# Decay factors loaded as rows, three small loads moved, and the last squares taken in place, in a hybrid gMLP and state-space decoder kernel

## The chip, the cores and the metric

The kernel runs on one core of a Trainium2 chip. The metric is the device time of one execution in microseconds; of the kernel before, three runs took 1399.7 to 1400.92 us, with a median of 1400.12 us. A separate execution with the hardware profiler gives the profile.

## The reference, cut to what matters

One layer works on x of 1024 tokens by 1024 features, all in float32. A conditioning vector c gives a shift, a scale and a gate. The normalized and modulated input h is multiplied by `w_in` (1024 x 11296), and its columns feed two branches: a gMLP branch (y_a) and a Mamba-2 state-space branch (y_b). The branches are projected, gated, added and projected once more.

```python
adt = dt * a                                   # per token and head, 32 heads
a_cs = jnp.cumsum(adt, axis=-1)                # within chunks of 128 tokens
decay = segsum_exp(adt)                        # exp(a_cs[i] - a_cs[j]) for i >= j, else 0
cb = jnp.einsum('bclgn,bcsgn->bcgls', cc, bc)
y_diag = jnp.einsum('bcgls,bcgrls,bcsgrp->bclgrp', cb, decay, xd)
...
y_off = jnp.einsum('bclgn,bcgrpn,bcgrl->bclgrp', cc, prev_states, jnp.exp(a_cs))
return (y_diag + y_off).reshape(b, s, h, p).astype(x.dtype)
...
y_b = y_b + xh * d_skip[:, None]
yz = (y_b.reshape(b, s, SSM_D_INNER) * jax.nn.silu(ssm_z)).reshape(b, s, SSM_GROUPS, ...)
y_b = rms_norm(yz, ssm_norm_w.reshape(SSM_GROUPS, -1)).reshape(b, s, SSM_D_INNER)
merged = jax.nn.sigmoid(g_a) * (y_a @ w_proj_a) + jax.nn.sigmoid(g_b) * (y_b @ w_proj_b)
return x + gate[:, None, :] * (merged @ w_out)   # then a last rms_norm
```

The `jnp.exp(a_cs)` in `y_off` is what the change is about: one number per token and head, by which the part of y that comes from the state is multiplied.

## The kernel before, in words

The kernel is written as a sequence of stages in which TensorE is to be fed without a break. Large products are cut into quadrants (seven products in place of eight), and each float32 operand is split into a high part (a cast) and a low part (a subtraction), so that each product is made three times. A framework places the instructions of the engines: what is wrapped in `pin` (`tc.keep_in_program_order`) keeps its order on its engine; everything else is put by the framework's own schedule where it expects the operands to be ready, be it much earlier than the place in the code. Each engine then works strictly in its order. Loads go out from SyncE (`load`, L89, in program order), stores from ScalarE's queue (`store`, L92). A tile that takes the place of an older one (same tag) waits until all readers of the older one are through.

The stages, with their times in the profile:

1. **First products (0 to 73 us).** For n = 0 to 7 the kernel makes a column block of the modulation (`matvec`, L254, from the weights `aw`), transposes x, and makes the rows of h: `modulation` (L271 to 278) adds on VectorE, `rows_of_h` (L287) on ScalarE, and `first_products` (L322) multiplies them on TensorE. At n = 1, `dtb`, `abc` and `dsk` are loaded (L457 to 460): 32 numbers each, broadcast to 128 partitions. `dsk` is first needed in `small_parameters2` (L495), which copies it into `dskt` (L503); `dtb` and `abc` in the dt part, near 690 us. Which task runs when is written as slots: `later(25, small_parameters)` (L1268) means 25 products on.
2. **The projections (73 to 918 us).** `v_block` and then pairs of column blocks of `w_in`. Beside them, in small tasks, the softplus of dt and the sums are made (`dt_part1` to `dt_part3`, L641 to 717). `dt_part3` puts the running sums a_cs, heads on partitions, into `act` (32 x 1024) and stores them in DRAM as `acs_d`.
3. **The state-space stage (918 to 1146 us).** There are 32 steps: 8 groups of 4 heads by 4 pieces of 256 tokens, in the order of L1241. For a step, `fetch` (L1080) loads `dcy`, the sums of the 4 heads broadcast to all partitions, and `sl` (B, C, x and z of the piece), into one of 5 sets of buffers. `decay` (L1096) first makes `ea` = exp of the sums on ScalarE (L1101, two instructions of 64 partitions, heads of even and of odd number), then masks `dcy` in place on GpSimd (L1104), then takes 8 exponentials (L1109). `prep` makes transposes and the products with the decay (L1129), `front` multiplies (`yi`, `sp`) and carries the state `st` on (L1157 on GpSimd, L1159 on VectorE), and `back` multiplies the state (`yn`) and lets `evacuate` (L1176) put y together: `ym` = `yn` x `ea` (L1189), then on GpSimd the sum (L1190) and the product with z (`yz`, L1191). Between these, TensorE is filled with pieces of y_a times `w_proj_a` (`proj_a`, L1397): a generator, of which `draw(n)` takes n pieces of two matmuls, 192 in all, 24 for a block of rows. Its weights are cast (`wah`, L1316) and subtracted (`wal`, L1317) beside it. A step's order is front, draws, back, prep of two steps on, fetch of six on, decay of four on (L1461 to 1471).
4. **The norm of y_b.** `post` (L1193) stores `yz` in DRAM and, for most groups, squares it five slots later (`squares`, in place) and sums over channels with the matmuls `pq` in `post2` (L1213). For the second half of the last two groups it squares at once into new tiles `sq` (L1203), whose tags are those of `ea` (`ea_r`) and of `ym` or `y1`. Their `post2` stands behind `draw(left[0] - 5)` (L1477 to 1479), when 5 pieces of `proj_a` are left.
5. **Projection of y_b (from 1160 us).** Units (`p1`, k) and so on, L1532. A unit has `loads` (a norm row `rb`, `yn` = y_b from DRAM, weights `p1r`), `operands` (norm, cast, subtraction on VectorE and ScalarE) and `multiply` (L1585): 12 matmuls into 4 PSUM banks x0 to x3 or y0 to y3. `loads` of six units and `operands` of four run ahead (L1681). The first `rb` tile takes the first tag of `ea_r` (L1480, L1515 to 1517), the first `yn` tiles take tags of the state and of `proj_a`'s operands. The banks take the places of those of the stage before, in the order of L1709.
6. **The last product with `w_out`, the residual and the final norm (to 1403 us).**

## Time and profile before

| | |
|---|---|
| median of 3 runs | 1400.12 us |
| the profiled execution | 1404.41 us, of which its span is 1402.7 us |
| mean granted TensorE clock | 0.993 |
| TensorE, VectorE, ScalarE, GpSimd busy | 98%, 74%, 57%, 13% of the span |
| moved by DMA | 288.60 MB, 206 GB/s over the span |

In the rows, PE is TensorE (PEld its weight loads), DVE VectorE, ACT ScalarE, POOL GpSimd, SP SyncE; ACTq and SPq are the queues from which an engine issues DMAs. "L1104" is a line of the kernel. A row of the timeline has a start and a length in us, the engine, the line, output and inputs by name, shapes, and in brackets how long the engine stood idle before and what ended that. A row of the waits has the engine, its instruction, the instruction or DMA it waited for, and then the sum in us, the number of times and the longest. A row of the windows view has the stretch, its length, and for PE, PEld, DVE, ACT and POOL the busy time with the number of instructions, then the granted clock, the DMA engines' share and GB/s. A row of groups or of a tile has durations in ns. A busy TensorE is not one at its peak: at a granted clock of 0.5 it is as busy and half as fast.

### The profile page before, as it was taken

Reading aid. Unit: us, or ns where it says so; the run is one execution under the profiler, and the core shown is the slowest. Engines: PE = TensorE matmul, PEld = TensorE weight load, DVE = VectorE, ACT = ScalarE, POOL = GpSimd, SP = SyncE. Lnnn points to the kernel's source line nnn. Section 1 sums busy time; section 2 is a strip of 40 time slices with the busy share of each in tenths; the row PEclk is TensorE's granted clock in tenths of the full one; section 3 lists DMA queues with packets and bytes.
Section 4 is the critical chain, followed back from the end, with each engine's and each line's share of the span. In section 5 each row is a group of like instructions: output and inputs, shape, how many; then the busy total and the mean of one; then the engine's idle time right before and its main releaser. Section 6 shows DMA issues by size and latency. Waiting matters only on the chain.

```text
span 1402.7 us, 20203 instructions
## 1 busy us (share of the span) xinstructions
PE 1370.8 (98%) x6951; PEld 1133.6 (81%) x6951; DVE 1041.7 (74%) x1724; ACT 800.0 (57%) x1447; POOL 189.1 (13%) x191
## 2 busy tenths in 40 slices
PE   8999999999999999999999999999999999999997
PEld 6588888888888888888888888888888877788786
DVE  4685876777778789788888885398777736859976
ACT  4664666667556566465576555677666714233443
POOL 1000000000000000000000000038868760000002
PEclk9999999999999999999999999999999999999999
DMA  8674534343435667787675764698787719978913
GB/s 265 176 234 137 151 120 121 100 126 118 130 99 148 195 196 246 229 260 210 196 218 177 234 205 139 212 362 305 270 272 266 266 65 323 346 250 298 381 63 120
DMA packets 247228, 288.60 MB, mean 206 GB/s; under 512 B 14509, under 2 KB 194133, under 8 KB 247125
## 3 DMA queue, kind: packets, MB, share of 16 engines
q1 hardware_dynamic: 173716, 203.76, 45.5%
q10 hardware_dynamic: 73408, 83.54, 17.5%
q8 instruction: 55, 0.90, 0.3%
q14 instruction: 49, 0.39, 0.1%
HBM read 199.79 MB, written 87.46 MB: 205 GB/s over the span
## 4 chain that ended last, share of the span: by engine, by line
PE 69%; DMA 11%; DVE 8%; ACT 4%; issue 3%; SPq 2%; POOL 2%; ACTq 0%; DVEq 0%; POOLq 0%
PE xz L565 6%; PE xx L565 6%; PE xg L565 5%; PE xcb L565 5%; PE xuz L565 5%; PE pma L81 3%; PE vx L954 3%; PE yx L565 3%; PE yz L565 3%; PE ycb L565 3%; PE yg L565 3%; PE ox L1775 2%; PE yuz L565 2%; SPq L90 2%; DMA yn<-yb_d 2%
## 5 line engine op out<-in xcount | busy, mean ns | idle before, releaser
L1104 POOL TENSOR_SCALAR_AFFINE_SELECT dcy<-dcy 128x1024 f32<-128x1024 f32 x32 | 35.0, 1092 | 794.6 <-DMA yl<-ya_d 748.6
L1109 ACT ACTIVATE dcy<-dcy,nacs 128x128 f32<-128x128 f32 x256 | 78.5, 388 | 14.1 <-POOL dcy L1104 13.7
L1101 ACT ACTIVATE ea<-dcy 64x512 f32<-64x512 f32 x64 | 40.1, 626 | 13.0 <-DMA dcy<-acs_d 12.5
L1189 DVE TENSOR_TENSOR ym<-yn,ea 128x512 f32<-128x512 f32 (+1 forms) x32 | 19.9, 622 | 32.8 <-PE yn L81 32.8
L81 PE MATMUL pma<-yh,wah 128*128 128x512 f32 x128 | 43.9, 424 | 0.0
L1129 DVE TENSOR_TENSOR dcy<-dcy,pc 128x1024 f32<-128x1024 f32 x32 | 38.9, 1217 | 5.0 <-PE pc L84 4.0
L81 PE MATMUL pma<-yh,wal 128*128 128x512 f32 x128 | 42.6, 414 | 0.0
L1024 ACT ACTIVATE ac<-ac 128x1024 f32<-128x1024 f32 x32 | 34.0, 1061 | 13.5 <-DVE ac L1022 13.2
L1191 POOL TENSOR_TENSOR yz<-y,sl 128x512 f32<-128x512 f32 x32 | 41.4, 1293 | 0.9
L81 PE MATMUL pma<-yl,wah 128*128 128x512 f32 x128 | 40.3, 396 | 0.0
L1530 DVE SCALAR_TENSOR_TENSOR yn<-yn,par,rb 128x512 f32<-128x512 f32 x32 | 23.8, 747 | 21.7 <-DMA yn<-yb_d 21.7
L1190 POOL TENSOR_TENSOR y<-y,ym 128x512 f32<-128x512 f32 (+1 forms) x32 | 36.5, 1142 | 14.6 <-DVE ym L1189 14.6
L81 PEld LDWEIGHTS yn<-sl,st 128*128 128x128 f32 x224 | 30.2, 191 | 8.4 <-POOL yz L1211 2.5
L81 PE MATMUL sp<-xe,bn 128*128 128x256 f32 x112 | 33.7, 418 | 3.1 <-DVE ssq L1221 1.6
L81 PE MATMUL yi<-dcy,xd 128*64 128x128 f32 x512 | 35.9, 284 | 0.7 <-DVE st L1159 0.7
L81 PE MATMUL yn<-sl,st 128*128 128x128 f32 x224 | 31.1, 276 | 5.2 <-DVE st L1159 5.2
L1790 POOL TENSOR_TENSOR r<-r,fnw 128x512 f32<-128x512 f32 x4 | 5.3, 1334 | 228.6 <-ACT junk L1788 228.6
L1022 DVE SCALAR_TENSOR_TENSOR ac<-c2x,cwt,ac 128x1023 f32<-128x1023 f32 (+2 forms) x24 | 30.7, 1280 | 6.2 <-ACT ac L1020 6.1
L1022 DVE SCALAR_TENSOR_TENSOR ac<-c2cb,cwt,ac 128x1023 f32<-128x1023 f32 (+2 forms) x24 | 30.6, 1275 | 5.6 <-ACT ac L1020 5.5
L824 ACT CAST wbb<-wbr 128x512 fp32r<-128x512 f32 x32 | 19.8, 619 | 26.1 <-DMA wb_d<-wbb 20.5
L986 ACT ACTIVATE vm<-vm,vr 128x128 f32<-128x128 f32 x64 | 25.8, 484 | 14.9 <-DMA vm<-v_d 10.3
L1157 POOL TENSOR_TENSOR st<-st,cd 128x256 f32<-128x256 f32 x48 | 32.9, 685 | 9.7 <-PE yn L81 6.3
(2974 smaller groups left out, 4385.3 us busy)
## 6 DMA issues: line engine op xcount, KB each, us to landing
sl<-s_d SPq DMA_DIRECT2D x32, 768.0 KB
s_d<-ac ACTq DMA_DIRECT2D x32, 512.0 KB
wb_d<-wbb ACTq DMA_DIRECT2D x32, 512.0 KB
dcy<-acs_d SPq DMA_DIRECT2D x32, 512.0 KB
av<-in_w_in_dram SPq DMA_DIRECT2D x36, 256.0 KB
aw<-in_ada_w_dram SPq DMA_DIRECT2D x16, 512.0 KB
wbr<-in_w_proj_b_dram SPq DMA_DIRECT2D x32, 256.0 KB
yb_d<-yz ACTq DMA_DIRECT2D x32, 256.0 KB
```

The source lines that it names most:

```text
L81: pin(PE.matmul(acc, l, r, start=first, stop=last))
L565: pin(PE.matmul(ps, lw[:, k * P : (k + 1) * P], r[k], start=first and n + k == 0, stop=n == 2 and k == 3, skip_group_check=not first))
L954: pin(PE.matmul(ps[pn][j], l[:, j * P : (j + 1) * P], r, start=nm in ("p1", "p5", "p2") and n + units[i][1] == 0, stop=n == 2 and k == 3, ...
L1022: V.scalar_tensor_tensor(ac[:, s:], cc[:, : S - s], conv_wt[:, 3 - s, i : i + 1], ac[:, s:], op0=ALU.mult, op1=ALU.add)
L1024: A.activation(ac, ac, AF.Silu)
L1101: A.activation(ea[hh * HD : (hh + 1) * HD], dcy.rearrange("p (j e) i l -> p e j (i l)", e=2)[hh * HD : (hh + 1) * HD, hh], AF.Exp)
L1104: G.affine_select(out=d8, in_=d8, compare_op=ALU.is_ge, fill=-1e30, base=0, pattern=[[0, 2 * HPG], [1, P]], channel_multiplier=-1)
L1109: A.activation(dcy[:, h, i, :], dcy[:, h, i, :], AF.Exp, bias=sub[:, i, h : h + 1])
L1129: V.tensor_tensor(d3, d3, pc[:, 0:256].unsqueeze(1).to_broadcast([P, HPG, 256]), op=ALU.mult)
L1157: G.tensor_mul(v3(s2), v3(self.st), fac(cd, g, s)[:, i].unsqueeze(2).to_broadcast([P, HPG, HD]))
L1190: G.tensor_add(y1[:, :, t0:], y1[:, :, t0:], m[:, :, t0:])
L1191: G.tensor_mul(yz, y1, sl[:, 4:6])
```

## The change

It has four parts.

- The exponentials of the sums are made once: two tasks follow `dt_part3`. `dt_part4` takes the exponential of `act` in place (32 x 1024, one instruction), and `dt_part5` stores it in DRAM as `eas_d`, in 16 stores, sorted by even and odd heads. `fetch` loads each step's `ea` as two broadcast loads of 64 partitions x 512, behind `sl`; the two exponentials at the head of `decay` are gone.
- The loads of `dtb`, `abc` and `dsk` move from n = 1 of the first products to the head of `small_parameters`.
- The late squares are made in place in `yz`, five slots after `post`, and not in new tiles. `post2` of group 6 stands where 8 pieces of `proj_a` are left, ahead of the first loads of `p1`; that of group 7 stands where 3 are left, after the loads of the fourth unit and the operands of the second.
- The eight first PSUM banks of stage 5 are named in another order.

```diff
     acs_d = dt_([NG, 4, HPG, 256], "acs_d")
+    eas_d = dt_([NG, 4, 2, HPG // 2, 256], "eas_d")
...
-                if at == 1 and n == 1:
-                    load(dtb, dt_bias.to_broadcast([P, NH]))
-                    load(abc, a_log.to_broadcast([P, NH]))
-                    load(dsk, d_skip.to_broadcast([P, NH]))
...
     def small_parameters():

+        load(dtb, dt_bias.to_broadcast([P, NH]))
+        load(abc, a_log.to_broadcast([P, NH]))
+        load(dsk, d_skip.to_broadcast([P, NH]))
         pkb = wide("pkb").rearrange("p (i q) -> p i q", q=P)
...
+        later(2, dt_part4, act)
+
+    def dt_part4(act):
+        A.activation(act, act, AF.Exp)
+        later(2, dt_part5, act)
+
+    def dt_part5(act):
+        for g in range(NG):
+            for e in range(2):
+                store(eas_d[g, :, e].rearrange("s j t -> j s t"),
+                      act[HPG * g + e : HPG * (g + 1) : 2, :].rearrange("h (s t) -> h s t", s=4))
...
                 ea = turn(ea_r, f"ea{nm}", F32).rearrange("p (j t) -> p j t", j=2)
+            for hh in range(2):
+                load(ea[hh * HD : (hh + 1) * HD],
+                     eas_d[g, s, hh].rearrange("j t -> (j t)").unsqueeze(0).to_broadcast([HD, 512]))
             self.pre[s] = (sl, dcy, ea)
...
             sl, dcy, ea = self.pre[s]
-            for hh in range(2):
-                A.activation(ea[hh * HD : (hh + 1) * HD],
-                             dcy.rearrange("p (j e) i l -> p e j (i l)", e=2)[hh * HD : (hh + 1) * HD, hh], AF.Exp)
...
-                self.late = sq = [turn(r, f"sq{g}", F32) for r in (ea_r, (ym_r, y1_r)[g % 2])]
-                for j in range(2):
-                    pin(A.activation(sq[j], yz[:, j], AF.Square))
-                G.tensor_add(sq[0], sq[0], sq[1])
+                self.late = [yz[:, j] for j in range(2)]
+                later(5, self.late_squares)
+
+        def late_squares(self):
+            sq = self.late
+            for j in range(2):
+                pin(A.activation(sq[j], sq[j], AF.Square))
+            G.tensor_add(sq[0], sq[0], sq[1])
...
-    draw(left[0] - 5)
-    for late in groups[NG - 2 :]:
-        late.post2(1, late.late[:1])
     room.extend(ea_r[0] + [st_r[0][1]])
...
+    draw(left[0] - 8)
+    groups[6].post2(1, groups[6].late[:1])
     for u in range(LOAD):
         loads(u)
         if u > 1:
             operands(u - 2)
+        if u == 3:
+            draw(left[0] - 3)
+            groups[7].post2(1, groups[7].late[:1])
...
-                first = {t: psb.tile([P, 512], F32, name=f"{t}p", tag=f"b{t}") for t in ('y0', 'y2', 'x0', 'x1', 'y1', 'x2', 'y3', 'x3')}
+                first = {t: psb.tile([P, 512], F32, name=f"{t}p", tag=f"b{t}") for t in ('y2', 'y1', 'x0', 'x1', 'x2', 'x3', 'y0', 'y3')}
```

## The prediction

> **What bounds the kernel now.** I read the page first, then busy time by stage (one call of the windows view), the waits, and the timeline around each place where TensorE stands still.
>
> ```profile
> span 1402.7 us, 20203 instructions
> ...
> PE 1370.8 (98%) x6951; PEld 1133.6 (81%) x6951; DVE 1041.7 (74%) x1724; ACT 800.0 (57%) x1447; POOL 189.1 (13%) x191
> ```
>
> TensorE is busy for 98% of the span: 1402.7 - 1370.8 leaves 31.9 us of idle. The change takes no product away, so a gain can come only from those 31.9 us and from stretches in which matmuls run at a lower granted clock. So the question is which pauses the edits reach. By stage (length, busy us of PE, PEld, DVE, ACT, POOL, then granted clock, DMA share, GB/s):
>
> ```profile
> 36.00:72.00 36.00, 33.87 (x232) 21.59 (x233) 25.43 (x54) 26.07 (x47) 0.00 (x0) 0.95 0.60 178
> ...
> 120.00:882.00 762.00, 761.37 (x3423) 629.83 (x3422) 591.50 (x923) 460.42 (x712) 1.30 (x2) 1.00 0.57 173
> ...
> 918.00:960.00 42.00, 41.95 (x292) 35.07 (x291) 35.92 (x61) 31.29 (x80) 23.20 (x25) 1.00 0.94 327
> 960.00:1000.00 40.00, 39.37 (x299) 34.36 (x298) 31.20 (x56) 32.46 (x86) 32.78 (x32) 1.00 0.82 289
> 1000.00:1040.00 40.00, 36.52 (x277) 32.25 (x276) 28.55 (x55) 25.63 (x65) 29.86 (x29) 0.96 0.75 253
> 1040.00:1080.00 40.00, 37.53 (x286) 32.50 (x286) 28.62 (x53) 26.92 (x72) 34.29 (x35) 1.00 0.81 282
> 1080.00:1120.00 40.00, 38.71 (x304) 34.06 (x303) 29.14 (x56) 28.05 (x73) 30.67 (x30) 1.00 0.83 286
> 1120.00:1140.00 20.00, 18.35 (x132) 15.53 (x130) 11.28 (x22) 2.51 (x5) 14.05 (x13) 0.91 0.07 26
> ...
> 1152.00:1162.00 10.00, 5.44 (x27) 3.98 (x27) 3.36 (x7) 2.27 (x4) 3.25 (x2) 0.81 0.74 253
> ...
> 1172.00:1182.00 10.00, 10.00 (x45) 8.24 (x45) 5.25 (x10) 2.36 (x5) 0.00 (x0) 1.00 0.81 258
> ```
>
> The projections (120 to 882) lose 0.6 us in 762: nothing is to be won there, and there is little to be seen if ACT gets more to do. Three places lose time: the first products (36 to 72: 2.1 us idle and a clock of 0.95), the state-space stage (918 to 1140: 0.05 + 0.63 + 3.48 + 2.47 + 1.29 + 1.65 = 9.6 us idle, and clocks of 0.96 and 0.91 in two windows), and the passage from `proj_a` to `p1` (1152 to 1162: 4.6 us idle, clock 0.81). The edits touch all three, so I price them one by one.
>
> **Edit A: the three small loads leave the first stage.** Start, length, engine, instruction, and what ended the idle time before it:
>
> ```profile
> 32.14 0.50 PE L81 MATMUL pm<-ones,row 128*128 128x1 f32 x4
> ...
> 36.28 0.35 DVE L503 COPY dskt<-dsk 64x16 f32<-64x16 f32 x2 [4.35 <-DMA dsk<-in_d_skip_dram]
> ...
> 37.86 0.73 PE L81 MATMUL acc<-b11h,w0h 128*128 128x512 f32 x2 [2.60 <-ACT b11h L300]
> ...
> 38.52 1.90 PE L81 MATMUL pm<-aw,scz 128*32 128x256 f32 x16
> ```
>
> ```profile
> 38.00:40.00 2.00, 2.00 (x18) 0.76 (x18) 1.45 (x3) 1.81 (x3) 0.00 (x0) 0.65 0.24 75
> 40.00:42.00 2.00, 2.00 (x10) 1.55 (x7) 1.81 (x4) 1.20 (x3) 0.00 (x0) 0.50 0.12 28
> ```
>
> VectorE's queue holds the copies `dskt<-dsk` (L503). The code asks for them far later, but they aren't kept in program order and stand here, in front of the modulation add (L275) of step n = 2. That add's input was there at 32.14 + 0.50 = 32.64. VectorE instead sat 4.35 us for the landing of `dsk`; behind it waited L275, ACT's `b11h`, and TensorE, which stood for 2.60 us. The next windows show a granted clock of 0.65 and 0.50: 2.0 x 0.35 + 2.0 x 0.50 = 1.7 us lost. With the loads gone, L275 can go at about 32.7, which is 4 us sooner, and `b11h` is ready by about 33.8, before TensorE is through with the products it has (35.26 = 37.86 - 2.60). So A is worth 2.60 + 1.7 = **4.3 us**. Bounds: 0, if another operand is late at the same place, and 4.3. I take the upper end, because ACT and VectorE move forward by the same 4 us and `w0` and `aw` for this step were already in use or landed. At their new place (ahead of `pkb`) the loads have no buffer to wait for, and the copies meet the projection stage, whose 0.6 us idle in 762 shows the cover; without it the price would be the 4.35 us again.
>
> By the Trainium skill, page "TensorE: Matmul & The Clock Gate", section "What's actually happening", the clock falls after an idle window of about 3.4 us; by that rule a 2.60 us pause costs nothing more, A would be 2.6 and the whole 1387. The trace disagrees (0.50 granted right behind a pause of 2.60), and I go by the trace.
>
> **Edit B: the squares of the last groups and the order around `p1`.**
>
> ```profile
> SPq L90 <- PE pq L81: 38.0, 1, 38.0
> ```
>
> ```profile
> 1152.67 0.32 SPq L90 DMA_DIRECT2D rb<-rs_d  x1
> ...
> 1155.30 0.63 PE L81 MATMUL pma<-yh,wal 128*128 128x512 f32 x2
> ...
> 1160.49 0.80 PE L1592 MATMUL x0p<-p1bh,p1a 128*128 128x512 f32 x1 [4.56 <-ACT p1a L1572]
> ...
> 1164.88 0.46 PE L1592 MATMUL x3p<-p1bh,p1a 128*128 128x512 f32 x1
> ```
>
> SyncE issues `rb<-rs_d`, the first load of `p1`, at 1152.67, after 38.0 us of waiting on the matmuls `pq`. The reason is a buffer: the first `rb` tile takes the first tag of `ea_r`, and the old code put the late squares `sq` there, which are read by `pq` at the very end. All of `p1`'s loads stand in line behind it. So TensorE ends `proj_a` at 1155.30 + 0.63 = 1155.93 and waits 4.56 us for `p1`'s first operands. Then the clock is down: each j of a unit has three products (L1590 to 1593), so the first `x3p` is the tenth, and nine took 1164.88 - 1160.49 = 4.39 us; at the rate of 1172 to 1182 (45 in 10 us, 0.222 each) they need 2.0. B costs 4.56 + 2.4 = **6.9 us** now.
>
> After the change the squares overwrite `yz`, the `ea_r` tags are free with the last `ym`, and the first loads hang on tags that `proj_a` gives back: `yh` of k = 0 in its last row block is read in the first 3 of 24 draws, so 21 draws of two products (21 x 2 x 0.222 = 9.3 us) before the end at least. From the first issue to `x0p` it takes 1160.49 - 1152.67 = 7.8 us now, so 9.3 do. What can be late next:
>
> ```profile
> L1205 ACT ACTIVATE sq<-yz x4: 615/623/631, 1140.1 to 1146.8; 128x512 f32<-128x512 f32 x4
> L1206 POOL TENSOR_TENSOR sq<-sq,sq x2: 1279/1283/1287, 1142.9 to 1147.5; 128x512 f32<-128x512 f32 x2
> ```
>
> The squares must now wait for the store of `yz` (behind them on ACT stand `p1`'s casts), then come 2 x 0.623 on ACT and 1.283 on POOL. They begin at 1140.1 and 1146.8 now, 15.8 and 9.1 us before 1155.93, and `pq` is asked for at 8 and 3 draws (3.6 and 1.3 us) before the end instead of 5: about 5 us are left for the later store. The subtractions of unit 0 on VectorE stand behind the first `pq`'s scaling (both kept in order); two of 0.69 (as that of L1317 below) fit in 3.6 us. The PSUM banks are renamed so that no `x` bank is one which `proj_a` still fills. I see nothing left to wait for and take 6.9; the bounds are 0 (another wait of the same length) and 6.9. The later units run at full rate already (10.00 busy of 10.00).
>
> **Edit C: `ea` comes by DMA.**
>
> ```profile
> L1101 ACT ACTIVATE ea<-dcy 64x512 f32<-64x512 f32 x64 | 40.1, 626 | 13.0 <-DMA dcy<-acs_d 12.5
> ```
>
> ```profile
> POOL dcy L1104 <- ACT ea L1101: 46.0, 20, 16.6
> ...
> ACT ea L1101 <- DMA dcy<-acs_d: 12.5, 9, 2.5
> ...
> PE yn L81 <- DVE st L1159: 5.2, 3, 2.4
> ```
>
> Removed: 64 exponentials of 626 ns, 40.1 us of ACT, 1.25 us per step of 32. POOL's mask (L1104) stands behind both, since it overwrites what they read: it waited 46.0 us for them in 20 cases (16.6 of that in one). Now it waits only for the load of `dcy`, for which ACT waited 12.5 us in 9 cases. None of that is on TensorE's path by itself. What reaches TensorE is the order within ACT, and two of its pauses (of the three behind `st`, 5.2 us together) show it:
>
> ```profile
> 996.81 0.69 DVE L1317 TENSOR_TENSOR wal<-wa,wah 128x512 fp32r<-128x512 f32 x1 [1.65 <-ACT wah L1316]
> ...
> 1002.02 0.68 PE L81 MATMUL yn<-sl,st 128*128 128x128 f32 x4 [1.13 <-DVE st L1159]
> ```
>
> ```profile
> 1072.47 1.26 ACT L1101 ACTIVATE ea<-dcy 64x512 f32<-64x512 f32 x2
> ...
> 1074.93 0.76 DVE L1317 TENSOR_TENSOR wal<-wa,wah 128x512 fp32r<-128x512 f32 x1 [2.14 <-ACT wah L1316]
> ...
> 1079.61 0.57 PE L81 MATMUL yn<-sl,st 128*128 128x128 f32 x3 [1.69 <-DVE st L1159]
> ```
>
> At 1074.93 VectorE waits 2.14 us for the cast `wah`, which stood on ACT behind the two `ea` of 1072.47 (1.26 us); the update `st`, queued behind it on VectorE, then lets TensorE wait 1.69 us. At 996.81 it is the same with 1.65 and 1.13 us. With ACT 1.26 us earlier both nearly vanish: 1.13 + 1.26 = 2.4 us at least. The rest of the 9.6 us are pauses of 0.6 to 2.4 us in which ACT has a part, or none; I count a quarter of it (7.2 x 0.25 = 1.8) and none of the clock loss (40 x 0.04 + 20 x 0.09 = 3.4). C gains about **4 us**. Bounds: everything, 9.6 + 3.4 = 13.0, and below nothing, since transfers are added.
>
> Added: two loads of 128 KB a step, a kind that before doesn't have, 8.4 MB in all. Their price is bounded by nothing (hidden) and by what rival 5 asks; the nearest rows give the middle. At 286 GB/s with DMA busy for 0.83 of the time, a full queue moves 345 GB/s, so a step's two loads cost 0.76 us of DMA in a step of about 6.9 us, and the share goes from about 0.8 to 0.91. For issues, and for the single steps near 750:
>
> ```profile
> L93 ACTq DMA_DIRECT2D acs_d<-act x8: 253/366/748, 745.1 to 748.7; - x8
> ```
>
> ```profile
> 748.59 1.28 ACT L1024 ACT_TABLE_LOAD   x1 [0.52 <-DMA acs_d<-act]
> ...
> 749.88 1.06 ACT L1024 ACTIVATE ac<-ac 128x1024 f32<-128x1024 f32 x1
> ```
>
> SyncE issues 64 more, at ACT's 0.366 each 23 us, on a queue that mostly waits for buffers here. `ym` on VectorE now needs that load and no longer ACT; behind it would wait `st` and the next `dcy` product. A new `ea` waits for the `ym` of five steps before; the `sl` load just ahead of it waits for POOL's `yz` of that step, which follows `ym`, so no wait is added, but the next `dcy` load is behind two more issues and 0.76 us of transfer. It has cover: the mask leads its products by 20 us and more (rows in rival 5).
>
> Once: an exponential of 32 x 1024 on ACT (1.06 us for the same length), up to two table loads of 1.28, and 16 stores at 0.366, 5.9 us. The 8 stores of `acs_d` (745.1 to 748.7) left no mark on TensorE in that stage. I take 0; without the cover it is 5.9 + 1.06 + 2.56 = 9.5.
>
> **Sum.** 4.3 + 6.9 + 4 = 15.2 us. The profiled execution took 1404.41 us (span 1402.7, 1.7 around it), so it would take 1389.2. The median of the runs shown, 1400.12, lies 4.3 us lower; I take the sum from it: **1385 us**. About 0.2% (2.8 us) is what a measurement of this kernel can tell from no change.
>
> **Rivals.**
> (1) C gives nothing or a little less than nothing, since the freed ACT time is off TensorE's path and the order of unpinned work is drawn up anew: 1400.1 - 11.2 = 1389, up to 1393 with new pauses of 4 us. For it: VectorE and POOL, not ACT, are behind the longest pauses. Chance 0.27.
> (2) C gives nearly all of it, as fewer pauses also cost less clock: 1400.1 - 11.2 - 11 = 1378. For it: the windows of 0.96 and 0.91 are those with pauses. Against: of the idle time 1.65 us lie behind 1120, when the last mask (1112.4), and so the last `ea`, is over. Chance 0.12.
> (3) B trades one wait for another (store of `yz`, square, sum, `pq`, all on the in-order queues of ACT, POOL, VectorE and TensorE): 1385 + 6.9 = 1392. Against: the 5 us worked out above. Chance 0.09.
> (4) A does not do what it says: the copies of `dsk` block VectorE at another place: 1385 + 4.3 = 1389. Chance 0.05.
> (5) Slower: the `ea` loads in front of the next `dcy` load make POOL's mask wait in each step. POOL is in order, with `st`, `y` and `yz` behind the mask.
>
> ```profile
> L81 PE MATMUL yi<-dcy,xd x512: 272/273/476, 920.8 to 1136.6; 128*64 128x128 f32 x171
> ...
> L1104 POOL TENSOR_SCALAR_AFFINE_SELECT dcy<-dcy x32: 1088/1092/1102, 900.2 to 1112.4; 128x1024 f32<-128x1024 f32 x32
> ```
>
> 32 steps in (1136.6 - 920.8)/31 = 6.96 us each. POOL is busy (32.78 + 29.86 + 34.29 + 30.67)/160 = 0.80 of it, 5.6 us, so it has 1.4 to spare. Beyond a wait of 1.4 us a step it sets the pace; from 1.4 + 11.2/31 = 1.8 us on the gains of A and B are eaten up. If each step waits as long as the longest wait for `dcy` now, 2.5 us, the stage is 31 x 1.1 = 34 us longer: 1400 - 11 + 34 = 1423. Against: the last mask begins at 1112.4 and its products end at 1136.6, a lead of three steps. Chance 0.06.
>
> The Trainium skill speaks for this last one: "DMA: Bandwidth & Descriptors", section "Rules for kernel authors", says that two transfers to disjoint halves of the partitions serialize and should be one of 128 partitions; the two `ea` loads are just that. No row of before shows a half-partition load.
>
> **How the numbers follow.** Forecast 0.41, the rivals 0.27, 0.12, 0.09, 0.05, 0.06. The range 1377 to 1395 takes in all but the slower case and the tails. Faster by over 0.2% is 0.91 (all but rival 5 and some of the tail of 1), the same 0.03, slower 0.06.
>
> **What would show it.** A: no pause of TensorE near 35 to 38 and a granted clock of 1.00 from 38 to 42. B: SyncE issues `rb` some 10 us before the end of `proj_a`, and the first `x0p` follows `pma` without a pause at full clock. C: no L1101 on ACT, the wait of L1104 on `dcy<-acs_d` alone and well under 46 us, waits of `wal` on `wah` shorter, fewer pauses of `yn`; DMA share about 0.91 in 960 to 1120. The prediction is wrong if L1104 waits on DMA in most steps, if `x0p` shows a new releaser, or if the stage from 918 to 1140 is no shorter.

## The result, and the profile after

The changed kernel takes 1387.26 us (median of four runs, 1387.07 to 1389.31), where the kernel before takes 1400.52 us in the same comparison (1399.7 to 1402.12): a ratio of 0.9907, with a 95% interval of 0.989 to 0.9924. The forecast was 1385 us, its range 1377 to 1395. The profiled execution took 1389.31 us with a span of 1387.6, at a mean granted clock of 0.997.

First the page of the changed kernel (span, then each engine's busy time, share and instructions):

```profile
span 1387.6 us, 20280 instructions
...
PE 1364.9 (98%) x6951; PEld 1131.6 (82%) x6951; DVE 1041.7 (75%) x1724; ACT 764.4 (55%) x1386; POOL 193.1 (14%) x191
```

TensorE's idle time is 1387.6 - 1364.9 = 22.7 us, 9.2 less than the 31.9 before. ScalarE has lost 35.6 us of work (800.0 to 764.4). Line numbers are higher in the changed kernel: `yi` is L82, the mask L1115, the exponentials of `dcy` L1120, `wah` L1331, `wal` L1332.

Next the same stretches as before (length, busy us of PE, PEld, DVE, ACT, POOL, granted clock, DMA share, GB/s):

```profile
36.00:72.00 36.00, 35.69 (x235) 23.73 (x235) 26.56 (x53) 27.44 (x50) 0.00 (x0) 1.00 0.60 176
38.00:40.00 2.00, 1.98 (x10) 1.39 (x10) 1.35 (x4) 1.15 (x2) 0.00 (x0) 1.00 0.98 283
...
120.00:882.00 762.00, 761.88 (x3430) 631.29 (x3429) 591.26 (x923) 464.37 (x717) 1.74 (x2) 1.00 0.56 173
918.00:960.00 42.00, 38.44 (x245) 31.95 (x245) 27.47 (x50) 21.00 (x61) 21.38 (x23) 0.92 1.01 312
960.00:1000.00 40.00, 39.37 (x305) 34.26 (x302) 32.17 (x58) 21.85 (x64) 33.03 (x33) 1.00 0.97 325
1000.00:1040.00 40.00, 40.00 (x313) 35.30 (x312) 30.67 (x60) 23.39 (x71) 34.53 (x33) 1.00 0.96 316
1040.00:1080.00 40.00, 36.79 (x289) 32.08 (x288) 28.96 (x52) 18.66 (x54) 33.59 (x33) 1.00 0.96 322
1080.00:1120.00 40.00, 38.47 (x304) 34.04 (x303) 30.13 (x57) 20.74 (x62) 30.34 (x30) 1.00 0.95 320
...
1152.00:1162.00 10.00, 10.00 (x47) 8.03 (x46) 10.00 (x18) 3.34 (x6) 2.02 (x1) 1.00 0.68 229
```

Edit A shows in the second row and edit B in the last: both at a clock of 1.00, where 0.65 and 0.81 stood, and 1152 to 1162 has no idle time left. The state-space stage in between is another matter. Its windows from 960 to 1120 have 39.37 + 40.00 + 36.79 + 38.47 = 154.6 us of products, against 152.1 before. But 918 to 960, in which TensorE had lost 0.05 us, now loses 3.56 us and runs at 0.92. So C gives in the middle of the stage and takes at its head. Measured from the first `yi` to the last, the stage is longer than before:

```profile
L82 PE MATMUL yi<-dcy,xd x512: 272/273/476, 914.6 to 1132.1; 128*64 128x128 f32 x171
```

It takes 1132.1 - 914.6 = 217.5 us, and took 1136.6 - 920.8 = 215.8.

The timeline shows the passage into `p1` and the stage's two large pauses:

```profile
948.88 1.19 PE L82 MATMUL yn<-sl,st 128*128 128x128 f32 x4 [2.82 <-DVE st L1170]
...
1075.84 0.68 PE L82 MATMUL yn<-sl,st 128*128 128x128 f32 x4 [2.65 <-POOL yz L1202]
...
1150.78 0.62 PE L82 MATMUL pma<-yh,wal 128*128 128x512 f32 x2
1151.23 0.40 PE L1604 MATMUL x0p<-p1bh,p1a 128*128 128x512 f32 x1
```

`x0p` follows the last `pma` without a pause, as B was to bring about. The pause of 2.82 us at 948.88 is new, and it is followed by a stretch at half clock (below). Behind which waits do they stand? Columns: engine, tile and line that waited, for what, then the sum in us, the number and the longest; from 918 to 1140:

```profile
ACT dcy L1120 <- POOL dcy L1115: 33.9, 19, 4.2
...
POOL dcy L1115 <- DMA dcy<-acs_d: 24.4, 14, 4.9
...
DVE wal L1332 <- ACT wah L1331: 12.2, 8, 4.9
...
ACT wah L1331 <- PE sp L82: 7.9, 1, 7.9
```

The same stretch of the kernel before:

```profile
POOL dcy L1104 <- ACT ea L1101: 42.3, 19, 16.6
...
ACT dcy L1109 <- POOL dcy L1104: 13.1, 15, 1.7
...
DVE wal L1317 <- ACT wah L1316: 7.8, 6, 2.1
```

GpSimd's mask no longer waits for ScalarE's `ea` (42.3 us) but for the landing of `dcy` (24.4 us, 14 times). ScalarE, freed of `ea`, waits 33.9 us for the mask, where it had waited 13.1. And one cast `wah` waited 7.9 us: VectorE's `wal` stood 4.89 us for it, with `st` behind it, and TensorE's `yn` 2.82 us for `st`. So the waits of `wal` on `wah`, which were to become shorter, went from 7.8 to 12.2 us, and 6.6 of these fall into 918 to 960.

### The profile page after: what moved, and what is told of

Read it like the earlier page. It is cut to its first block, busy times and chain, and to the rows that moved or that the text cites. A ratio compares the mean times of both kernels' runs of the same rounds, so it can differ in the third digit from the quotient of the medians.

```text
span 1387.6 us, 20280 instructions
## 1 busy us (share of the span) xinstructions
PE 1364.9 (98%) x6951; PEld 1131.6 (82%) x6951; DVE 1041.7 (75%) x1724; ACT 764.4 (55%) x1386; POOL 193.1 (14%) x191
## 4 chain that ended last, share of the span: by engine, by line
PE 89%; DVE 3%; DMA 2%; POOL 2%; ACT 1%; issue 1%; SPq 1%; POOLq 0%; ACTq 0%; DVEq 0%
PE xcb L565 6%; PE xz L565 6%; PE xx L565 6%; PE xuz L565 6%; PE xg L565 6%; PE pma L82 5%; PE ox L1792 3%; PE yx L565 3%; PE ycb L565 3%; PE vx L965 3%; PE yp L1604 3%; PE yz L565 3%; PE yuz L565 3%; PE yg L565 3%; PE yi L82 2%; PE sp L82 2%
## 5 line engine op out<-in xcount | busy, mean ns | idle before, releaser
L1115 POOL TENSOR_SCALAR_AFFINE_SELECT dcy<-dcy 128x1024 f32<-128x1024 f32 x32 | 38.1, 1192 | 790.0 <-DMA dcy<-acs_d 787.9
L1120 ACT ACTIVATE dcy<-dcy,nacs 128x128 f32<-128x128 f32 x256 | 79.1, 389 | 45.0 <-POOL dcy L1115 33.9
L82 PE MATMUL pma<-yh,wah 128*128 128x512 f32 x128 | 43.5, 421 | 0.0
L82 PE MATMUL pma<-yh,wal 128*128 128x512 f32 x128 | 42.6, 414 | 0.0
L82 PE MATMUL pma<-yl,wah 128*128 128x512 f32 x128 | 40.3, 396 | 0.0
L1035 ACT ACTIVATE ac<-ac 128x1024 f32<-128x1024 f32 x32 | 33.9, 1061 | 10.9 <-DVE ac L1033 10.7
L82 PEld LDWEIGHTS yn<-sl,st 128*128 128x128 f32 x224 | 30.8, 193 | 10.9 <-POOL yz L1202 6.0
L82 PE MATMUL yn<-sl,st 128*128 128x128 f32 x224 | 32.5, 280 | 6.9 <-DVE st L1170 4.2
L82 PE MATMUL yi<-dcy,xd 128*64 128x128 f32 x512 | 35.9, 284 | 1.5 <-DVE st L1170 1.5
L82 PE MATMUL sp<-xe,bn 128*128 128x256 f32 x112 | 33.1, 413 | 2.2 <-DVE xe L1136 2.2
L82 PEld LDWEIGHTS yi<-dcy,xd 128*64 128x64 f32 x512 | 28.0, 139 | 5.7 <-issue 2.4
```

The source lines that it names most:

```text
L82: pin(PE.matmul(acc, l, r, start=first, stop=last))
L1035: A.activation(ac, ac, AF.Silu)
L1115: G.affine_select(out=d8, in_=d8, compare_op=ALU.is_ge, fill=-1e30, base=0, pattern=[[0, 2 * HPG], [1, P]], channel_multiplier=-1)
L1120: A.activation(dcy[:, h, i, :], dcy[:, h, i, :], AF.Exp, bias=sub[:, i, h : h + 1])
```

## The experiments

Twelve kernels, five rounds each, in three groups; the ratio is to the kernel before, run beside them on the same chip. In the middle columns are figures from the profiled execution: the first `vx` (what A moves), first to last `yi`, TensorE's busy time from 918 to 960 and from 960 to 1120, and from the last `yi` to the first `x0p` of `p6` (the passage that B changes).

| kernel | median us | ratio (95%) | first vx | yi | 918-960 | 960-1120 | last yi to p6 |
|---|---|---|---|---|---|---|---|
| before | | 1 | 73.1 | 215.8 | 41.95 | 152.13 | 70.5 |
| changed, first comparison | 1387.26 | 0.9907 (0.989 to 0.9924) | 68.2 | 217.5 | 38.44 | 154.63 | 63.0 |
| e1: without C | 1392.63 | 0.9938 (0.9922 to 0.9955) | 68.4 | 213.2 | 41.95 | 150.44 | 69.1 |
| e2: C alone | 1399.73 | 0.9993 (0.9979 to 1.0006) | 72.0 | 214.0 | 38.78 | 155.81 | 72.4 |
| e3: B alone | 1396.31 | 0.9964 (0.9951 to 0.9978) | 72.0 | 213.6 | 41.95 | 153.21 | 69.9 |
| e4: ea kept | 1401.59 | 1.0003 (0.9991 to 1.0014) | 68.4 | 221.2 | 41.95 | 151.93 | 71.0 |
| e5: changed, again | 1389.61 | 0.9921 (0.9905 to 0.9937) | 68.3 | 213.8 | 39.45 | 155.53 | 63.1 |
| e6: without C, old banks | 1386.74 | 0.9900 (0.9883 to 0.9918) | 68.5 | 215.3 | 41.95 | 149.93 | 63.0 |
| e7: changed, old banks | 1389.98 | 0.9927 (0.9912 to 0.9942) | 68.7 | 218.3 | 38.04 | 154.22 | 64.1 |
| e8: one load, rows of 2 | 1503.97 | 1.0747 (1.0728 to 1.0766) | 68.5 | 327.8 | 32.74 | 119.01 | 63.2 |
| e9: half the bytes | 1391.17 | 0.9933 (0.9917 to 0.9949) | 72.1 | 218.7 | 41.92 | 149.35 | 63.0 |
| e10: half on ScalarE | 1392.26 | 0.9944 (0.9926 to 0.9963) | 68.4 | 220.3 | 41.40 | 152.01 | 63.0 |
| e11: ea later | 1388.89 | 0.9922 (0.9907 to 0.9936) | 68.2 | 215.6 | 38.60 | 154.75 | 63.0 |
| e12: one load, rows of 16 | 1395.14 | 0.9963 (0.9948 to 0.9978) | 68.4 | 211.0 | 42.00 | 155.67 | 63.0 |

The theory at the start, from the profile above: A and B make the whole gain, and the loads of `ea` take back what they free. The rivals: C gives the 4 us of the forecast; C costs.

### e1, without C, and e6, the same with the old order of the banks

e1 puts back the old `decay` and takes the loads, `eas_d` and its two tasks out:

```diff
-            for hh in range(2):
-                load(ea[hh * HD : (hh + 1) * HD],
-                     eas_d[g, s, hh].rearrange("j t -> (j t)").unsqueeze(0).to_broadcast([HD, 512]))
...
+            for hh in range(2):
+                A.activation(ea[hh * HD : (hh + 1) * HD],
+                             dcy.rearrange("p (j e) i l -> p e j (i l)", e=2)[hh * HD : (hh + 1) * HD, hh], AF.Exp)
```

> The changed kernel without its loads of ea: the small loads are moved and the late squares are in place, but ea is made by ScalarE in each step, as before. Theory (the two other parts make the whole gain, and in the loads the time that ScalarE is freed of comes back as waits on DMA): 1387 us, within 1.5 of the changed kernel's 1387.26; the state-space stage (first to last yi) takes 215.8 us as before and not the 217.5 of the changed kernel, and the passage into p1 stays without a pause. Rival 1 (the loads of ea do give the 4 us of the forecast, seen elsewhere than in that stage): 1391. Rival 2 (the loads cost more than they give): 1384 to 1385.

It took 1392.63 us, not 1387, which speaks for rival 1. But the stage is shorter than that of the changed kernel (213.2 against 217.5), and the passage longer, with a pause that nobody had expected. The timeline of e1:

```profile
1149.27 0.39 PE L1592 MATMUL x1p<-p1bh,p1a 128*128 128x512 f32 x1
1153.76 0.50 PE L1592 MATMUL x2p<-p1bh,p1a 128*128 128x512 f32 x1 [4.10 <-DVE tha L1423]
```

`x2p` waits for `tha`, VectorE's reading of the last `pma`. The compiled programs say why. Without C the last two `pma` lie in PSUM banks 4 and 0, with C in 6 and 1; the order in which the code asks for banks is the same, but the framework gives them out by its own schedule, and C changes that. The new order of names puts x0 to x3 into 2, 3, 4 and 5, so without C `x2` lands on a bank that is still being read, and on VectorE `tha` stands behind a row of operands. The old order puts them into 2, 3, 5 and 7. e6 is e1 with that one line as before:

```diff
-('y2', 'y1', 'x0', 'x1', 'x2', 'x3', 'y0', 'y3')
+('y0', 'y2', 'x0', 'x1', 'y1', 'x2', 'y3', 'x3')
```

> The small loads moved and the late squares in place, ea made by ScalarE, and the eight banks named in the old order. In the run without the loads of ea but with the new bank order, x2p waited 4.10 us for tha: the last two pma lay in banks 4 and 0 there (6 and 1 in the changed kernel), and the new order puts x2 into bank 4; the old order puts the x into 2, 3, 5 and 7. Theory (the loads of ea give nothing of themselves; they only move the pma to other banks, and each bank order fits one of the two): no pause at p1, 1392.6 - 4.1 - 1.7 = 1386.8 us, the same as the changed kernel within 1.5. Rival (the loads of ea give 4 to 5 us by what they take from ScalarE, and the bank is a detail): 1391 to 1393.

1386.74 us; the passage is 63.0 us and the pause is gone. The two kernels are 5.9 us apart in their medians and 5.3 by the ratios (they ran in different groups), and 6.1 us in the passage (69.1 to 63.0). So A and B without C are as fast as the whole change, and the rival falls: what looked like a gain of C in e1 was a clash of banks.

### e5 and e7, the changed kernel again, and with the old order of the banks

> The changed kernel once more, beside the three others on one chip, so that a few us can be told. Both theories: 1387.3 us within 1.5, no pause of TensorE between the last pma and the second unit of p1.

> The changed kernel with the eight banks in the old order: one line undone. x3 then lies in bank 7, which the last pq holds until VectorE has scaled it (at 1154.25 in the changed kernel, where the first x3p started at 1153.29), and y2 (the row pr6) in bank 1, that of a pma which tha reads at 1156.2 to 1157.5. Theory (banks that the stage before still holds make TensorE wait): a pause of about 1 us at x3p and about 2 us at pr6 (2.01 was there in the run with the loads of ea alone), with some clock loss: 1389 to 1392 us. Rival (the order of the banks is of no consequence where the loads of ea are): 1387.3.

e5 took 1389.61 us, 0.8 us beyond the 1.5 allowed, and e6 beside it 1386.74: C costs 2.9 us by the medians, with intervals that overlap (0.9905 to 0.9937 and 0.9883 to 0.9918). e7 took 1389.98, so here the order of the banks makes no difference that the runs can tell (0.4 us). In its profile the passage is 1.0 us longer, with the pause foretold at `x3p`, of 0.77 us, but none at pr6:

```profile
1155.88 0.50 PE L1604 MATMUL x3p<-p1bh,p1a 128*128 128x512 f32 x1 [0.77 <-DVE ssq L1236]
```

### e2, C alone, and e3, B alone

e2 adds the loads of `ea` to the kernel before, with nothing else (the hunks of the diff with `eas_d`, `dt_part4`, `dt_part5`, `fetch` and `decay`); e3 adds only the squares in place, the order around `p1` and the order of the banks (the other hunks but for the three small loads).

> The kernel before with the loads of ea alone; the small loads stand at n = 1 and the late squares in tiles of their own, as before. Theory (they give nothing): 1400.5 within 1.5, first to last yi 216 to 217.5 us, and the pauses of 2.60 us (first products) and 4.56 us (before x0p) are there as before. Rival 1 (4 us by fewer pauses): 1396.5. Rival 2 (they cost): 1402 to 1404. A further possibility: the first rb still takes a tag of ea with the late squares, so the passage into p1 must stay as it is; if it gets shorter here, it is not the squares that held it.

> The kernel before with the late squares in place, the new order around p1 and the new order of the banks alone. Theory: the passage into p1 gives 7 us and the units behind it some 2 to 3 more, since loads and operands run further ahead (the pauses of 1.36 and 0.57 us there are gone): 1391 us, x0p directly behind the last pma. Rival (the part is worth only the 6.9 us of the passage, and what was gained behind it belongs to the loads of ea): 1393.6, with the later pauses still there.

e2: 1399.73 us, a ratio of 0.9993 whose interval holds 1: C alone gives nothing that can be told, as the theory had it, though its stage took 214.0 us and not the 216 to 217.5 expected. Its x0p has a pause of 3.50 us and pr6 one of 2.01, so the passage was not mended by the freed `ea` tags. e3: 1396.31 us, 5.3 us above the theory and 2.7 above the rival, so neither held. It has e1's clash, and a passage of 69.9 us:

```profile
1157.85 0.79 PE L1593 MATMUL x2p<-p1bh,p1a 128*128 128x512 f32 x1 [3.87 <-DVE tha L1424]
```

e1 and e3 differ by A alone and ran side by side: A is worth 1396.31 - 1392.63 = 3.7 us. A run of A by itself was not made, nor one of B by itself with banks that fit.

### e4, the loads of ea left out after the first five steps

```diff
+            if nstep[0] > NSET:
+                self.pre[s] = (sl, dcy, kept_ea[n])
+                return
```

> The changed kernel, but only the first five steps load ea; the 27 others multiply by the factors of these five, so the output's factors are wrong on those steps and 7 MB of loads are left out. ScalarE is freed of the exponentials all the same. Theory (the freed time is worth a few us, and the loads take it back by coming late): first to last yi 213 to 214 us, the mask's wait for dcy below 12 us where the changed kernel has 24.4, DMA share 0.80 to 0.85 in 960 to 1120, and 1383 to 1384 us. Rival (the freed time lies off TensorE's path and is worth nothing even when nothing is loaded): 1387, with 216 us or more for the stage, though the waits for dcy are short.

1401.59 us: both were wrong, though the rival had the length of the stage on its side. The mask's wait for `dcy` in 918 to 1140 is 27.9 us, no less than with the loads. The last `pma` went to banks 2 and 0 this time, and `x0p` is in bank 2:

```profile
1162.94 0.76 PE L1608 MATMUL x0p<-p1bh,p1a 128*128 128x512 f32 x1 [5.64 <-DVE tha L1439]
```

The stage takes 221.2 us with ScalarE as free as in the changed kernel. So the freed ScalarE alone does not shorten the stage, and the mask's wait is not the work of the loads of `ea`. In e8 to e12 the names of the banks were fitted to where the last `pma` fell.

### e9, e10 and e11: bytes, a mixture, and the order of the loads

e9 loads half the columns of `ea`, e10 half of the partitions (and makes the other half on ScalarE), e11 asks for `ea` two steps later (`EA_BEHIND` is 2). In this order:

```diff
-                load(ea[hh * HD : (hh + 1) * HD],
-                     eas_d[g, s, hh].rearrange("j t -> (j t)").unsqueeze(0).to_broadcast([HD, 512]))
+                load(ea[hh * HD : (hh + 1) * HD, 0],
+                     eas_d[g, s, hh, 0].unsqueeze(0).to_broadcast([HD, 256]))
```

```diff
+            load(ea[0:HD], eas_d[g, s, 0].rearrange("j t -> (j t)").unsqueeze(0).to_broadcast([HD, 512]))
...
+            A.activation(ea[HD:P], dcy.rearrange("p (j e) i l -> p e j (i l)", e=2)[HD:P, 1], AF.Exp)
```

```diff
+            waiting.append((self, s, n))
+            while len(waiting) > (EA_BEHIND if nstep[0] < 4 * NG else 0):
+                of, at, m = waiting.pop(0)
+                of.fetch_ea(at, m)
```

> The changed kernel, but each of the two loads of ea brings only 256 of its 512 columns, and ym uses them for both halves of the channels: the factors of every second pair of heads are left out, the number of loads stays, their bytes are halved. The banks are fitted to where the last pma fall here (2 and 1). Theory (what ScalarE gives is taken back because the loads fill the DMA engines and the sums for the mask come late): the mask waits about 12 us for dcy in place of 24, the DMA share in 960 to 1120 is 0.90 in place of 0.97, first to last yi 212 to 214 us, and 1385 us or less where the changed kernel takes 1387.3 to 1389.6. Rival (the order into which the framework puts the engines' work is what moves the stage, and the bytes are of no consequence): 214 to 218 us for the stage and 1387 to 1390, though the mask waits less.

> The changed kernel with half of ea loaded (64 partitions, heads of even number) and half made by ScalarE as before; the banks are fitted to where the last pma fall here (2 and 0). Theory (DMA bytes against ScalarE time): half the relief at half the bytes, the mask waits for ScalarE and for dcy about 12 us each, and 1386 us, a little below both the changed kernel and the one with ea all on ScalarE (1386.7). Rival (neither is on TensorE's path): 1386.7 to 1389.6, within what the two already span.

> The changed kernel with the loads of ea asked for two steps later, behind dcy and sl of the second next step: the same bytes, but what the mask waits for goes first. Banks fitted (the last pma in 2 and 1). Theory, if the price of the loads is that they stand ahead of the next dcy: the mask's wait for dcy falls from 24 us to under 15, first to last yi 213 to 215 us, and 1385 to 1387 us. Rival (it is the full DMA engines, in whatever order): waits of 20 us and more, and 1387 to 1390.

The waits for `dcy` in 918 to 1140, first of e9, then of e11:

```profile
POOL dcy L1115 <- DMA dcy<-acs_d: 29.9, 14, 8.1
```

```profile
POOL dcy L1123 <- DMA dcy<-acs_d: 29.7, 17, 7.9
```

Neither half the bytes nor a later place in the queue shortens the mask's wait (24.4 us in the changed kernel), and no stage comes out at 212 to 214 us. e9 took 1391.17, but its profiled execution lost 3.8 us before `vx` (72.1 against 68.3), ahead of anything that the edit touches; e10 took 1392.26, and its mask waited 32.8 us for the half of `ea` that ScalarE makes, where 12 us for ScalarE and 12 for `dcy` were expected; e11 took 1388.89. So e9 and e10 lie above both their views. e11 has the numbers of its rival, but the reason given there (full DMA engines) does not fit e9, where the DMA share is 0.88 and the wait no shorter. The theory that the loads take C's gain back through the mask falls.

The table's two columns show where it goes instead. In the five kernels with two full loads of `ea` a step (changed, e2, e5, e7, e11) the middle has 154.2 to 155.8 us of products, and in the four with `ea` on ScalarE (before, e1, e3, e6) 149.9 to 153.2: means of 155.0 and 151.4, so 3.6 us are won there. At the head the same five lose 2.5 to 4.0 us where the other four lose 0.05. The sum of both, with the clock behind the head's pause, is a stage of 215.8 us on average with the loads and 214.5 without. In each of the five, and in none of the others, one `wah` in that stretch waits 6.8 to 8.3 us. In e5:

```profile
ACT wah L1331 <- DMA dcy<-acs_d: 6.8, 1, 6.8
```

Four of the five profiles name a DMA for it (`dcy`, `sl`), that of the changed kernel's first comparison TensorE's `sp`. What holds the cast up stands in front of it on ScalarE: the issue of a store, `mt_d<-tha` (a finished block of `proj_a`). First VectorE's `tha`, then ScalarE's queue, then a load of SyncE, all in the changed kernel:

```profile
936.40 1.27 DVE L1435 SCALAR_TENSOR_TENSOR tha<-tha,pma 128x512 f32<-128x512 f32 x2
```

```profile
934.71 0.37 ACT L1142 COPY bn<-pc 128x256 f32<-128x256 f32 x1 [1.10 <-DVE dcy L1140]
942.57 0.33 ACTq L1437 DMA_DIRECT2D mt_d<-tha  x1
943.02 0.62 ACT L1331 CAST wah<-wa 128x512 fp32r<-128x512 f32 x1 [7.94 <-PE sp L82]
```

```profile
933.05 0.32 SPq L91 DMA_DIRECT2D sl<-s_d  x1
```

And in e6:

```profile
932.47 0.68 DVE L1423 SCALAR_TENSOR_TENSOR tha<-tha,pma 128x512 f32<-128x512 f32 x1
...
933.18 1.69 ACTq L1425 DMA_DIRECT2D mt_d<-tha  x2
```

In e6 the store goes out as soon as the first `tha` is there. In the changed kernel both `tha` are done at 937.67, and the store goes out at 942.57. A landing is reported by a semaphore, a counter for which an engine can wait, and the trace keeps these events: ScalarE's wait in front of the store was for a semaphore, and ended 0.02 us after the last count of that one, which came at 942.50. That count is the landing of the `sl` load issued at 933.05, and the store then uses the same semaphore for itself. The cast's own load was no hindrance: the first `wa` of its pair, issued at 928.11, had landed at 935.72. It is so in all five kernels: the store shares its semaphore with an `sl` load, which takes 8.8 to 9.8 us from issue to landing. In the nine others the store's semaphore was last used by a load other than `sl` (`tha`, in e4 `wa`), and in six of them (before, e1, e3, e4, e6, e10) the store goes out within 0.04 us of `tha`.

So at the head ScalarE stands for a load that neither the store nor the cast needs. Which load shares a semaphore with the store differs from kernel to kernel, as the banks do; that it is `sl` in just the five kernels with two full loads of `ea` is what the traces show, not why. The pause does not go with the bytes alone: e9 and e10 load half and have 41.92 and 41.40 us of products at the head, but e12, below, loads as much as the five, and its store waits for a `tha` (it also begins the stage later).

The gain in the middle is made of the waits that the prediction had named: from 960 to 1120 `yn` waits 0.2 to 1.2 us for `st` in the five kernels and 5.0 to 5.3 in the four with `ea` on ScalarE, and `wal` 3.5 to 5.9 us for `wah` against 7.0 to 8.7; a new pause of 2.7 to 2.8 us behind `yz` takes part of it back in four of the five (that at 1075.84 above). But the freed ScalarE alone does not bring it: e4 has no gain there, nor have e9 and e10, and in e4 `yn` waits 5.2 us for `st`. Nor is it excluded that the pause at the head, during which other engines go on, takes waits out of the middle; e12, which has the gain without that pause, speaks against it, but begins later. Why the middle gains in some kernels and not in others is open: the framework draws up the unpinned work of ScalarE, VectorE and GpSimd anew for each of them. A changed kernel whose stores of `mt_d` stand behind the casts, or share no semaphore with `sl`, would show what C is worth without the pause at the head; it was not run.

### e8 and e12, one load of ea in place of two

```diff
-            for hh in range(2):
-                load(ea[hh * HD : (hh + 1) * HD],
-                     eas_d[g, s, hh].rearrange("j t -> (j t)").unsqueeze(0).to_broadcast([HD, 512]))
+            load(ea, eas_d[g, s].rearrange("e j t -> e (j t)").unsqueeze(1).to_broadcast([2, HD, 512]))
```

e12 loads from a copy that holds each row eight times: `eas_d[g, s].rearrange("e c j t -> (e c) (j t)").unsqueeze(1).to_broadcast([16, 8, 512])`.

> The changed kernel with one load of ea a step over all 128 partitions (256 KB) in place of two of 64 partitions; the framework puts the last pma into banks 3 and 0 here, so the order of the banks is fitted to that (x in 2, 4, 5 and 6). By the Trainium skill, DMA: Bandwidth & Descriptors, section Rules for kernel authors, two transfers to disjoint halves of the partitions serialize and should be one. Rival (that is what the loads cost): the mask waits for dcy well under the 24.4 us of the changed kernel, say 12, the stage from first to last yi is 213 to 215 us, and the time 1383 to 1385. Theory (it is the bytes: the DMA engines are at a share of 0.95 or more either way): waits for dcy of 20 us and more, share 0.95, and 1387 within 2.

> One load of ea a step over all 128 partitions as in the run that took 1504 us, with the same banks, but from a copy in DRAM that holds each row eight times, so that the load's outermost dimension is 16 (each row then goes to 8 partitions) and not 2. For this dt_part5 makes 64 stores in eight tasks in place of 16. Theory (the 115 us came from the outermost dimension of 2, by which a load of 256 KB used few of the DMA engines: their share fell to 0.61 to 0.68 while all waited for loads): share 0.95 again in 960 to 1120, first to last yi 214 to 218 us, 1387 to 1390. Rival 1 (two loads of half the partitions cost more than one of all): 1384 to 1385. Rival 2 (one large load of ea in the queue is itself what holds up the others): well over 1400.

From 960 to 1120, e8 and then e12:

```profile
960.00:1120.00 160.00, 119.01 (x747) 99.87 (x746) 76.19 (x140) 54.09 (x162) 80.91 (x80) 0.86 0.63 207
```

```profile
960.00:1120.00 160.00, 155.67 (x1205) 136.59 (x1204) 122.11 (x225) 89.09 (x267) 130.70 (x129) 1.00 0.98 335
```

e8 took 1503.97 us: the same bytes in one instruction made each step (327.8 - 213.8) / 31 = 3.7 us longer than in e5, and the mean DMA share fell to 0.63 while the mask waited 115.4 us for `dcy` between 900 and 1140. With an outermost dimension of 16 (e12) the share is 0.98 again. That agrees with what the Trainium skill, "DMA: Bandwidth & Descriptors", section "Rules for kernel authors", states elsewhere in that table: an outermost dimension of c < 16 confines a DMA to at most c engines. My expectation for e8 had overlooked this rule, and both its views were wrong.

e12 has the shortest stage of all, 211.0 us, with 42.00 and 155.67 us of products, and a mask that waits 9.5 us for `dcy` (beside one wait of 26.0 us for `px` at the head). The shorter stage is on the side of rival 1, and of the advice that e8 went by (the Trainium skill, "DMA: Bandwidth & Descriptors", section "Rules for kernel authors": one transfer of 128 partitions in place of two halves), but the time fits none of the three views. It is no proof either: its stage began 11.3 us later than e5's (first `pma` at 924.1 against 912.8), since the 64 stores on ScalarE's queue held up the projections, and so the first loads had more time. In the timeline of e12, first ScalarE, whose `ac` waits for one of these stores, then TensorE:

```profile
804.83 1.24 ACT L1033 ACTIVATE ac<-c1cb,par,cwt 128x1024 f32<-128x1024 f32 x1 [5.42 <-DMA eas_d<-act]
805.97 0.56 ACT L581 COPY c2cb<-xcb 128x512 f32<-128x512 f32 x1
```

```profile
806.59 2.07 PE L565 MATMUL xcb<-t4h,p4cb7h 128*128 128x512 f32 x4 [7.99 <-ACT c2cb L581]
...
829.30 1.19 PE L565 MATMUL xz<-t4h,p4z5h 128*128 128x512 f32 x4 [1.32 <-ACT c2z L581]
```

From the first `vx` to the first `pma` it took 855.7 us, against 844.5 in e5; hence 1395.14 us in all. A cheaper way to make the copy was not run.

## Why the prediction was right

- **What bounds the kernel** held: everything won was a pause of TensorE or the clock behind it.
- **A**, forecast 4.3 us: right in mechanism (no pause, clock 1.00), 4.9 us between the two profiles and 3.7 between e1 and e3.
- **B**, forecast 6.9 us: the pause is gone, and the stretch from the last `yi` to `p6` is 70.5 - 63.0 = 7.5 us shorter. The step on the PSUM banks was right for a reason that I had not seen. With the allocation of the kernel before, the old order of names was free of clashes and the new one costs 6 us (e1); C moves the last `pma`, and only there does the new order fit. The banks are a joint of B and C, not a detail of B. In time, the 12.5 us of e6 less the 3.7 of A leave 8.8 for B, more than the 6.9 (from two groups of runs).
- **C**, forecast 4 us: this step failed. The middle of the stage did win 3.6 us, near the 2.4 + 1.8 of the working, and in the waits of `yn` and `wal` that it had named; but since e4, e9 and e10 have ScalarE freed in whole or in half and no such gain, it is not shown that the freed time brings it, and the agreement in size may be luck. What failed is "so no wait is added": I followed `dcy`, `sl` and `ea` to the instructions that use them, and not to the store `mt_d<-tha`, in front of which ScalarE stands until an `sl` has landed. The head of the stage loses 2.5 to 4.0 us and in four of the five profiles 1.7 to 3.4 more to the clock. The DMA share was put too low as well, at 0.91, where it is 0.95 to 0.97. A and B without C take 1386.74 us beside 1389.61 with it: C gives nothing or costs some 3 us. That is rival 1 (1389, up to 1393), not the forecast. The prediction had named as a sign of being wrong that the stage is no shorter: from 215.8 us it went to 217.5 in the first profile and to 213.8 in the second (e5).
- **The step beside 750**, costed at nothing: right for 16 stores, though each takes 0.597 us to issue and not 0.366. First `vx` to first `pma` is 843.4 and 844.5 us with them (changed, e5), 844.4 and 843.6 without (e1, e6). With 64 (e12) the cover is gone.
- **The sum**: 15.2 forecast, 13.3 measured. That they are so near is partly luck: A and B gave 1399.28 - 1386.74 = 12.5 us in e6 where 11.2 were forecast, and this hides a C that gave none of its 4. By the time alone 1387.26 lies no nearer to the forecast (1385) than to rivals 1 and 4 (1389). The two profiles differ by 15.1, which looks better than it is: 2.1 us of it lie behind the first `x0p` of `p7` (151.1 us to the end before, 149.0 after), and e2, which changes nothing there, has 149.0 as well. The profiled execution of the kernel before was a bad one, 4 us above its median.
- **Rival 5** (the mask sets the pace) did not come: 24.4 us of waiting in 32 steps, 0.8 a step, are under the 1.4 us worked out as its spare. The wait of the mask was the wrong place to look for the price.

## What to carry to other kernels

Taking work from an engine that is not the bound pays only through the waits that reach the bound; when the work goes to the DMA queue instead, list everything that waits for a landing, also the stores that an engine has to issue before it can go on, and look at the stage's head, where many loads are due at once. An order of buffers or banks that is fitted by hand to a scheduler's allocation belongs to one program: after any edit, compare the allocation again, since a clash costs nearly half of what the edit was worth (here 6 us of 13). The same holds for the semaphores that DMAs share. And give a broadcast load an outermost dimension that is large (here 16 against 2: a DMA share of 0.98 against 0.63).

## What the runs showed of the hardware

The half clock comes in pieces. The windows around the pause of the changed kernel at 948.88, and then e9 near 28 us, where the longest pause since 4 us had been one of 0.59 (TensorE was busy for 1.28 us of 22.00 to 24.00):

```profile
946.00:948.00 2.00, 0.06 (x1) 0.00 (x0) 2.00 (x5) 0.54 (x2) 2.00 (x3) 1.00 1.01 316
948.00:950.00 2.00, 1.12 (x5) 1.16 (x6) 0.73 (x3) 0.81 (x3) 1.73 (x3) 0.56 0.91 206
...
952.00:954.00 2.00, 2.00 (x17) 1.58 (x16) 2.00 (x3) 0.58 (x2) 2.00 (x4) 0.50 1.03 402
954.00:956.00 2.00, 2.00 (x9) 1.65 (x8) 1.38 (x4) 2.00 (x8) 1.00 (x1) 0.74 0.87 334
956.00:958.00 2.00, 2.00 (x14) 1.75 (x12) 0.11 (x1) 1.29 (x3) 0.00 (x0) 1.00 0.88 193
```

```profile
24.00:26.00 2.00, 1.58 (x18) 1.08 (x21) 1.16 (x3) 1.21 (x2) 0.00 (x0) 0.90 0.89 250
26.00:28.00 2.00, 2.00 (x13) 1.22 (x5) 1.12 (x2) 0.91 (x3) 0.00 (x0) 0.50 0.82 177
28.00:30.00 2.00, 2.00 (x7) 1.71 (x7) 1.07 (x4) 1.18 (x2) 0.00 (x0) 0.50 0.99 281
30.00:32.00 2.00, 2.00 (x6) 1.41 (x6) 1.03 (x2) 0.67 (x2) 0.00 (x0) 0.50 0.99 279
32.00:34.00 2.00, 2.00 (x22) 1.22 (x21) 0.00 (x0) 1.22 (x2) 0.00 (x0) 0.90 0.06 20
```

In both, the clock is at 0.50 for about 6.8 us, so 3.4 us of work are lost. The pause of 2.65 us at 1075.84 in the changed kernel was not followed by any (1040 to 1080 and 1080 to 1120 have 1.00). The length of the pause alone does not say whether the clock falls: these runs show it after 0.59 us and not after 2.65. The Trainium skill, "TensorE: Matmul & The Clock Gate", section "What's actually happening", speaks of a free-running window of 3413 ns: 6.8 us are two of these, which agrees, and a window that runs on by itself would let the same pause count once and not another time. Its condition, one idle window of about 3.4 us, agrees with the pause of 2.65 us, and not with the other two places. This is one reason why the same stage code takes 213.8 to 217.5 us in two profiles of one kernel (changed and e5), and why a difference of 2 us in a single profile proves little here.
